# A two-layer hybrid encoder: interleaved softmax factors, tables and fetches moved, pools reordered

## The chip, the cores and the metric

The kernel runs on one NeuronCore of a Trainium2 chip. The metric is the device time of one execution in microseconds (us). Before the change it is 2843.03 us, the median of three runs (2841.9 to 2843.21).

## The reference

Input and output are 2048 × 1024 in float32. Two layers run one after the other, each with a residual. Cut to what matters:

```python
h = rms_norm(x, norm_g); proj = h @ w_in
# layer 0: two attentions over chunks of 64, 8 heads of 64 each
#   A: own chunk + 2 before, rope, a learned sink per head in the softmax
#   B: own chunk + 8 before, a relative-position bias added to the scores
x = x + concat([ya * silu(gate_a), yb * silu(gate_b)]) @ w_out
# layer 1: differential attention, 8 heads, keys up to the query's chunk
a = softmax(q1 @ k1.T * scale) - lam * softmax(q2 @ k2.T * scale)
o = rms_norm(a @ v, subln_g) * (1 - lambda_init)
x = x + (o * silu(gate)) @ w_out
```

## The kernel before, in words

Tokens are worked on in 16 tiles of 128, four of which make a block of 512. Matrix products of float32 quality are made from float32r halves: every operand is split into a high and a low part, and `mm3` (L209 to L217) issues three matmuls, high × high (L214), high × low (L215), low × high (L216). The low part of a weight is a subtraction on GpSimd (POOL, L310); for the first weights of layer 0, half of these subtractions run on VectorE (DVE).

`_project` computes a layer's q, k and v (layer 0: gates too) for two blocks at a time. `hidden` (L315) norms and transposes a block; layer 1 keeps one block in the pool `ev` and one in `hv`. `tables` (L264) loads cos and sin and calls `rope_tables` (L176), eleven DVE instructions (L185 to L193) that fold the gains into them. In layer 1 it is called at the start of the projection. Results go to scratch tensors in DRAM (q, k: L394, L395; v: L483), and the attention loads them again.

`_mix0` runs layer 0's attentions. `scores_a` (A) computes scores, sets masks by memsets (L632 to L634), takes the negated row maximum (L635) and its minimum with the sink (L636), then the exponential on ScalarE (ACT, L640), and adds the sink's term to the row sum (L643). `scores_b` (B) does the same with L716 to L724. The probabilities are transposed on TensorE (PE; L674, L739) into PSUM banks that `split_pt` (L591 on ACT, L592 on DVE) empties into halves, ahead of the products with v (L681, L683, L743, L744). `join` (L595) and `finish` (L602) merge heads and multiply by the gates (L605); `split_y` (L611, L612) splits the result. Some gates of layer 0 are computed in between, by `late_gate` (L775), whose tiles sg and gt share two buffers, tag `xr`, with the residual tiles of `out_tile` (L489). `out_tile` computes an output tile of 128 × 512 and adds the residual on DVE (L504).

`_mix1` runs layer 1's attention. `scores` (L892) works on key chunks of 512 and for both halves of the difference: L913 and L914 (PE), maximum (L917, DVE), exponential (L920, ACT). A row's chunks get factors e (L928) against their common maximum; e is multiplied by the chunk sums la (L929) and summed (L930). GpSimd scales and combines the probabilities (L936, L945, L946), with a part on DVE (L943). `values` (L949) transposes (L959), evacuates (L962 on ACT, L964 on DVE) and multiplies by v (L966). `gate` (L975) norms and gates the result. For the middle blocks o goes to DRAM, and `fetch` (L1016) loads it again (tile coy, L1020) and splits it at once (`split`, L1010: L1012 on ACT, L1013 on POOL). Output tiles: `out_begin` (L1075) loads the residual xr, `out_step` multiplies, `out_end` adds (L1088) and writes (L1089). The four-buffer tag `ot` holds gate outputs, o, coy and xr. `projected_last` does the last block's output, four tiles at a time, k by k.

Each engine runs its instructions in order, and so does SyncE (SP), which issues nearly all DMAs. The order is set when the kernel is built: generators (`pace`, `weave`) emit the heads, the products with v and the side work in turn; a list scheduler with its own timing model then places every instruction on its engine by readiness, and `issue_after` keeps an instruction behind a given one. Tiles come from pools; a tag's number of buffers decides how many lie side by side, and a pool that is opened later lies over one that was closed earlier, in the order of opening: in layer 1's attention `ot`, then `sm`, then `ld` (the q tiles, L888 and L889, and gate weights, L1059).

Of the kernel before, what the change touches and what calls it, by code (L numbers as in the profile page):

```python
# [85 lines left out]
class Trunk:  # L86
# [137 lines left out]
    def _project(self, es, layer):  # L224
# [39 lines left out]
        def tables():  # L264
            if layer == 0:
                self.parameters(xp.tile([P, D], F32, tag="xt", name=n + "tmp"))
            self.cos = xp.tile([P, S // P, 32], F32, tag="xt", name=n + "cos")
            self.sin = xp.tile([P, S // P, 32], F32, tag="xt", name=n + "sin")
# [3 lines left out]
            tabs["q"] = self.rope_tables(tb, self.gain[gq], 0.125, n + "tq")  # L272
            tabs["k"] = self.rope_tables(tb, self.gain[gk], 1.0, n + "tk")
# [145 lines left out]
        for half in range(2):  # L419
# [13 lines left out]
            for gi, (kind, c0, width, o) in enumerate(groups):  # L433
                w = ready or weights(c0, width)
# [54 lines left out]
    def out_tile(self, y, w, j, t, c, xin, xout, sb, pmm, n, tag, xtag="xr", xbufs=None, order=range(KT), after=None):  # L489

        nc = self.nc
        tok, cs = slice(t * P, (t + 1) * P), slice(c * 512, (c + 1) * 512)
        xr = sb.tile([P, 512], F32, tag=xtag, name=n + "xr", bufs=xbufs)
        nc.sync.dma_start(xr, xin[tok, cs])
        ps = pmm.tile([P, 512], F32, tag=tag, name=n + "om")
        for i, k in enumerate(order):
            self.mm3(
                ps, y[k][0][:, j * P:(j + 1) * P], y[k][1][:, j * P:(j + 1) * P],
                w[0][k][c], w[1][k][c], i == 0, i == KT - 1, self.anchor,
            )  # L500
            if after:
                after(i)
            yield 1
        nc.vector.tensor_tensor(xr, ps, xr, ALU.add)  # L504
        nc.sync.dma_start(xout[tok, cs], xr)
        yield 1
# [16 lines left out]
    def _mix0(self, es):  # L523
# [71 lines left out]
        def join(yt, O, e):  # L595
            hi = slice(e * HD, (e + 1) * HD)
            lo = slice((1 - e) * HD, (2 - e) * HD)
            tmp = sb.tile([P, BLK], F32, tag="low", name=n + "low")
            nc.scalar.activation(tmp[hi, :], O[lo, :], AF.Copy)
            nc.vector.tensor_tensor(yt[hi, :], O[hi, :], tmp[hi, :], ALU.add)  # L600
# [14 lines left out]
        def scores_a(h, b, res):  # L615
# [7 lines left out]
            for z in range(2):  # L623
# [12 lines left out]
                nc.vector.tensor_scalar(nm[:, zs], nm[:, zs], self.nsink[:, h:h + 1], None, ALU.min)  # L636
# [117 lines left out]
        def projected(b):  # L754
# [11 lines left out]
            for j, c in units:  # L766
                while next_load(c):
                    pass
                pm, tag = (pO, "O") if b == 0 and j % 2 else (pmm, "om")
                after = follow if b and (j, c) == units[-1] else None  # L770
                yield from self.out_tile(
                    split[b], w, j, b * NTB + j, c, a["x"], self.x1, yp, pm, n, tag, xbufs=2, order=ended, after=after
                )

        def late_gate(b, c, wg, h, r0):  # L775
# [7 lines left out]
            sg = yp.tile([P, BLK], F32, tag="xr", name=n + "sg", bufs=2)  # L783
# [73 lines left out]
    def _mix1(self, es):  # L857
        nc, tc, a, s = self.nc, self.tc, self.a, self.s1
        n = "c"
        pool = lambda nm, bufs, **kw: es.enter_context(tc.tile_pool(name=n + nm, bufs=bufs, **kw))  # L860
        ot = pool("ot", 4)
        sm = pool("sm", 8)
        ld = pool("ld", 2)
        yp = pool("y", 2 * KT)
        vp = pool("v", 4)
        pp = pool("pp", 20)
# [25 lines left out]
        def scores(h, b, q, K, res, then):  # L892
# [4 lines left out]
            for j in range(NTB):  # L897
# [5 lines left out]
                nm, la, e = small("nm", 8), small("la", 8), small("e", 8)  # L903
                nm, la, e = (x.rearrange("p (m z) -> p m z", m=2) for x in (nm, la, e))
                l, rl = small("l", 2), small("rl", 2)
                rows = []
                for m in range(2):
                    chunks = []
                    for z, (c, ce) in enumerate(cuts):
# [10 lines left out]
                        nc.scalar.activation(chunks[z][:, :wd], ps, AF.Exp, bias=nm[:, m, z:z + 1], accum_out=acc)  # L920
# [3 lines left out]
                if nb > 1:  # L924
# [4 lines left out]
                    nc.vector.tensor_tensor(pe, e[:, :, :nb], la[:, :, :nb], ALU.mult)  # L929
# [85 lines left out]

        def fetch(h, b):  # L1016
# [58 lines left out]
        def out_begin(b, j, c):  # L1075
# [3 lines left out]
            pl, tag = (pG, "G") if b < NB - 1 else (pS, "S")  # L1079
# [11 lines left out]
        def projected(b):  # L1091
# [3 lines left out]
            for i, c in enumerate(halves):  # L1095
                for j in range(NTB):
                    xr, ps, to = out_begin(b, j, c)
                    for k in range(KT):
                        out_step(b, j, k, ps, w)
                        if j == NTB - 1 and i == 0:  # L1100
                            load_w(halves[1], k, w[k])
                        elif j == NTB - 1:
                            fetch(k, b + 1)
# [4 lines left out]
        def projected_last():  # L1108
# [15 lines left out]
            for c, w in ((1, w[0]), (0, pairs)):  # L1124
                tiles = [out_begin(b, j, c) for j in range(NTB)]
                for k in range(KT):
                    while (k, b) not in ended:
                        yield 0
                    for j in range(NTB):
                        out_step(b, j, k, tiles[j][1], w)  # L1130
                    yield 1
                for t in tiles:
                    out_end(*t)
# [45 lines left out]
        def side():  # L1179
            yield from gates()  # L1180
            for b in range(NB):
                for h in range(8):
                    while (h, b) not in ended and b < NB - 1:
                        yield 0
                    fetch(h, b)
# [50 lines left out]
```

## Time and profile before

| | |
|---|---|
| median of three runs | 2843.03 us |
| the profiled execution | 2843.39 us |
| its span (first to last instruction) | 2841.6 us |
| TensorE busy | 2707.3 us, 95% |
| VectorE, GpSimd, ScalarE busy | 65%, 56%, 54% |
| mean granted TensorE clock | 0.987 |
| instructions | 43911 |
| moved by DMA | 521.68 MB, mean 184 GB/s |

The profile is one execution. "Busy" counts the time an engine spends in instructions; a stall of one engine is put down to the instruction whose end released it. A matmul that is waited for may run on a clock that the throttle has lowered, which the column of the granted clock shows (1.00 is full speed). In rows of the kind `2.56 POOL L612 ... x2` the first number is a length in us, the line is that of the kernel before, and the tile names are the program's. The stages of the span, by the lines that run in them: layer 0's projection to about 600 us, its attention and output to 1160, layer 1's projection to 1776, layer 1's attention and output to the end.

### The profile page before, as it was taken

To read this page: it belongs to the slowest core of one execution; us is meant where nothing else is said; L and a number is where in the kernel's file an instruction comes from. 1 tells how busy PE (TensorE), PEld (TensorE's weight loads), DVE (VectorE), ACT (ScalarE), POOL (GpSimd) and SP (SyncE) were. 2 spreads that over 40 slices of the span, in tenths; PEclk is the share of its full clock that TensorE was granted. 3 is DMA by queue.
4 is the path that set the end of the run, shared out by engine and by line. 5 is a ranking of instruction groups with operands and counts; after the bars stand their busy time and mean duration, and the time that the engine had idled before them with its cause. 6 is when DMAs were issued, how large, how long until landed. Compare 5 with 4: busy or idle time off the path is not lost.

```text
span 2841.6 us, 43911 instructions
## 1 busy us (share of the span) xinstructions
PE 2707.3 (95%) x13384; PEld 2171.4 (76%) x13384; DVE 1844.8 (65%) x4643; ACT 1543.8 (54%) x4015; POOL 1596.6 (56%) x1740
## 2 busy tenths in 40 slices
PE   7999999999899999899999999899999999999998
PEld 5888888887788888777788888777676777676766
DVE  7752285347788886498808870468787777666651
ACT  4443543367766666243334331468787676666751
POOL 3541252234545454267745560468888887888871
PEclk9999999999999999999999999999999999999999
DMA  5674343738887765476885443887868676464542
GB/s 161 228 233 149 108 140 120 220 117 232 218 197 186 190 181 150 155 271 198 254 255 189 141 126 108 251 251 212 248 187 232 180 212 207 120 191 131 176 137 81
DMA packets 356092, 521.68 MB, mean 184 GB/s; under 512 B 44816, under 2 KB 139792, under 8 KB 355856
## 3 DMA queue, kind: packets, MB, share of 16 engines
q1 hardware_dynamic: 355856, 518.87, 61.6%
q8 instruction: 107, 1.75, 0.3%
q14 instruction: 129, 1.06, 0.1%
HBM read 361.70 MB, written 157.02 MB: 183 GB/s over the span
## 4 chain that ended last, share of the span: by engine, by line
PE 73%; DVE 9%; DMA 9%; ACT 4%; issue 2%; POOL 2%; SPq 1%; DVEq 0%; ACTq 0%; POOLq 0%
PE cO L966 7%; PE p1mm L214 5%; PE p1mm L216 5%; PE p1mm L215 5%; PE cS L913 4%; PE cS L914 4%; PE ctr L959 3%; PE p0mm L214 3%; PE p0mm L216 3%; PE p0mm L215 3%; PE com L214 2%; PE com L215 2%; PE com L216 2%; PE mom L214 2%; PE cG L214 2%
## 5 line engine op out<-in xcount | busy, mean ns | idle before, releaser
L920 ACT ACTIVATE cP<-cS,cnm 128x512 f32<-128x512 f32 (+3 forms) x640 | 397.3, 628 | 181.6 <-DVE cnm L917 142.9
L917 DVE TENSOR_REDUCE cnm<-cS 128x1 f32<-128x512 f32 (+3 forms) x640 | 371.7, 601 | 80.0 <-PE cS L914 74.1
L936 POOL TENSOR_SCALAR cP<-cP,crl,ce 128x512 f32<-128x512 f32 (+3 forms) x288 | 220.0, 778 | 164.2 <-DVE crl L931 84.7
L215 PE MATMUL p1mm<-p1wL,p1hH 128*128 128x512 f32 x768 | 302.3, 394 | 0.4 <-POOL p1wL L310 0.4
L214 PE MATMUL p1mm<-p1wH,p1hH 128*128 128x512 f32 x768 | 301.1, 393 | 0.8 <-ACT p1wH L308 0.8
L216 PE MATMUL p1mm<-p1wH,p1hL 128*128 128x512 f32 x768 | 301.8, 393 | 0.0
L310 POOL TENSOR_TENSOR p0wL<-p0ws,p0wH 128x512 fp32r<-128x512 f32 (+1 forms) x124 | 149.4, 1237 | 266.8 <-ACT p0wH L308 257.8
L966 PE MATMUL cO<-cpt,cv 128*128 128x512 f32 (+3 forms) x640 | 287.7, 537 | 4.2 <-DVE cpt L964 3.6
L946 POOL TENSOR_TENSOR cP<-cP,cP 128x512 f32<-128x512 f32 (+3 forms) x256 | 285.5, 1140 | 1.4
L913 PE MATMUL cS<-ck,cqd 128*128 128x512 f32 (+3 forms) x640 | 261.2, 413 | 12.4 <-ACT cP L920 7.1
L214 PE MATMUL p0mm<-p0wH,p0hH 128*128 128x512 f32 (+1 forms) x640 | 239.9, 377 | 5.2 <-ACT p0vt L472 3.5
L310 POOL TENSOR_TENSOR p1wL<-p1ws,p1wH 128x512 fp32r<-128x512 f32 x128 | 169.2, 1342 | 133.6 <-ACT p1wH L308 126.4
L216 PE MATMUL p0mm<-p0wH,p0hL 128*128 128x512 f32 (+1 forms) x640 | 239.6, 375 | 1.8 <-DVE p0hL L336 1.8
L215 PE MATMUL p0mm<-p0wL,p0hH 128*128 128x512 f32 (+1 forms) x640 | 239.2, 374 | 0.0
L914 PE MATMUL cS<-ck,cql 128*128 128x512 f32 (+3 forms) x640 | 231.4, 367 | 4.4 <-DMA cql<-qL 4.4
L959 PEld LDWEIGHTS ctr<-ident,cP 128*128 128x128 f32 x1088 | 136.8, 141 | 109.7 <-issue 60.8
L945 POOL TENSOR_SCALAR cP<-cP,crl,ce 128x512 f32<-128x512 f32 (+3 forms) x230 | 180.0, 795 | 0.0
L959 PE MATMUL ctr<-ident,cP 128*128 128x128 f32 x1088 | 172.9, 274 | 0.8 <-ACT cpt L962 0.3
L214 PEld LDWEIGHTS p1mm<-p1wH,p1hH 128*128 128x128 f32 x768 | 144.7, 188 | 29.8 <-ACT p1wH L308 1.0
L215 PEld LDWEIGHTS p1mm<-p1wL,p1hH 128*128 128x128 f32 x768 | 144.7, 188 | 29.5 <-POOL p1wL L310 0.8
L216 PEld LDWEIGHTS p1mm<-p1wH,p1hL 128*128 128x128 f32 x768 | 144.7, 188 | 28.8
L913 PEld LDWEIGHTS cS<-ck,cqd 128*128 128x128 f32 x640 | 121.9, 191 | 44.6 <-ACT cP L920 19.9
(306 smaller groups left out, 7271.1 us busy)
## 6 DMA issues: line engine op xcount, KB each, us to landing
p1ws<-in_od_w_in_dram SPq DMA_DIRECT2D x56, 512.0 KB, 4.4
p0ws<-in_ev_w_in_dram SPq DMA_DIRECT2D x48, 512.0 KB, 4.4
ck<-kH SPq DMA_DIRECT2D x144, 128.0 KB, 3.3
ck<-kL SPq DMA_DIRECT2D x144, 128.0 KB, 3.5
cv<-v SPq DMA_DIRECT2D x72, 256.0 KB, 4.5
cqd<-qH SPq DMA_DIRECT2D x128, 128.0 KB, 4.6
cql<-qL SPq DMA_DIRECT2D x128, 128.0 KB, 4.6
cwH<-wgH SPq DMA_DIRECT2D x64, 256.0 KB, 4.6
```

What stands on the lines that cost most here:

```text
L214: mm(ps, aH, bH, start=first, stop=False)
L215: mm(ps, aH, bL, start=False, stop=False)
L216: mm(ps, aL, bH, start=False, stop=last)
L310: low.tensor_tensor(l[:, :width], ws[:, k, :width], f32(h[:, :width]), ALU.subtract)
L913: mm(ps, qd[:, m, js], kt[:, :wd], start=True, stop=False)
L914: self.anchor = mm(ps, ql[:, m, js], kt[:, :wd], start=False, stop=True).ins
L917: nc.vector.tensor_reduce(nm[:, m, z:z + 1], ps, AX.X, ALU.max, negate=True)
L920: nc.scalar.activation(chunks[z][:, :wd], ps, AF.Exp, bias=nm[:, m, z:z + 1], accum_out=acc)
L936: nc.gpsimd.tensor_scalar(p1, p1, rl[:, 0:1], e1, ALU.mult, ALU.mult)
L946: nc.gpsimd.tensor_tensor(p1, p1, p2, ALU.add)
L959: nc.tensor.transpose(tp[:, (j - j0) * P:(j - j0 + 1) * P], us[j][kt // 4][:, kk:kk + P], self.ident)
L966: mm(O[:, j0 * P:], v, T[:, :wd], start=(kt == 0), stop=(kt == nkt - 1), skip_group_check=True)
```

## The change

1. cos and sin lie in tag `xn` of pool `sb` (five buffers), no longer in the x tiles' tag `xt`. In layer 1 the table instructions are held behind the last residual add of layer 0.
2. The first weight group of layer 1 also has half its low parts subtracted on DVE.
3. L636 becomes two instructions of one column each. In layer 0, half of the output tiles of the last block take their residual tile from pool `yt`; sg has a buffer of its own, and `low` has one buffer, not two.
4. In layer 1's attention the pools open in the order `ld`, `sm`, `ot`, and `pp` (probabilities) has 19 buffers, not 20.
5. e and la lie in turn in one tile `el` of 16 columns, and the product is a reduction by multiplication over neighbours, so that it has one operand.
6. A fetched o lies in its own tag `oy` of two buffers; its split comes one fetch later and is held behind the latest exponential.
7. `projected_last` does seven of eight k of the four tiles of c = 1, seven of a tile of c = 0 "ahead", then the eighth k of both; the other three tiles follow one after another.
8. The side work waits for a head's end only where o went through DRAM.

```diff
+            self.cos = sb.tile([P, S // P, 32], F32, tag="xn", name=n + "cos", bufs=5)
...
+            with self.tc.issue_after(self.added) if layer else nullcontext():
+                tabs["q"] = self.rope_tables(tb, self.gain[gq], 0.125, n + "tq")
...
-                w = ready or weights(c0, width)
+                w = ready or weights(c0, width, first=half == gi == 0)
...
-        nc.vector.tensor_tensor(xr, ps, xr, ALU.add)
+        self.added = nc.vector.tensor_tensor(xr, ps, xr, ALU.add).ins
...
-                nc.vector.tensor_scalar(nm[:, zs], nm[:, zs], self.nsink[:, h:h + 1], None, ALU.min)
+                for j in (2 * z, 2 * z + 1):
+                    nc.vector.tensor_scalar(nm[:, j:j + 1], nm[:, j:j + 1], self.nsink[:, h:h + 1], None, ALU.min)
...
-            sg = yp.tile([P, BLK], F32, tag="xr", name=n + "sg", bufs=2)
+            sg = sb.tile([P, BLK], F32, tag="sg", name=n + "sg", bufs=1)
...
+        ld = pool("ld", 2)
+        sm = pool("sm", 8)
         ot = pool("ot", 4)
-        sm = pool("sm", 8)
-        ld = pool("ld", 2)
...
-        pp = pool("pp", 20)
+        pp = pool("pp", 19)
...
+                el = small("el", 16).rearrange("p (m z i) -> p m z i", m=2, i=2)
+                e, la = el[:, :, :, 0], el[:, :, :, 1]
...
-                    nc.vector.tensor_tensor(pe, e[:, :, :nb], la[:, :, :nb], ALU.mult)
+                    nc.vector.tensor_reduce(pe, el[:, :, :nb, :], AX.X, ALU.mult)
...
-                o = ot.tile([P, BLK], F32, tag="ot", name=n + "oy")
+                o = ot.tile([P, BLK], F32, tag="oy", name=n + "oy", bufs=2)
                 nc.sync.dma_start(o, s["o"][h * P:(h + 1) * P, b * BLK:(b + 1) * BLK])
-                split(h, b, o)
+                fetched.append((h, b, o))
+
+        def split_fetched(left):
+            if len(fetched) > left:
+                with tc.issue_after(self.exp):
+                    split(*fetched.pop(0))
...
+            first = [out_begin(b, j, 1) for j in range(NTB)]
+            for k in range(KT - 1):
+                yield from step(range(NTB), first, w[0], k)
+            ahead = [out_begin(b, 0, 0, pG, "G")]
+            for k in range(KT - 1):
+                yield from step((0,), ahead, pairs, k)
+            yield from step(range(NTB), first, w[0], KT - 1)
```

How this moves instructions is shown at three places; line numbers after the change are the same or higher, by up to 35. First, DVE in layer 0's attention A, where manm is the negated maximum, mSA the scores, mal the row sums and mptL a low half of transposed probabilities. Before:

```order
L634 MEMSET mSA 64x2x64
L635 TENSOR_REDUCE manm<-mSA 128x2
L633 MEMSET mSA 64x2x64
L636 TENSOR_SCALAR manm<-manm,nsink 128x2
L643 TENSOR_TENSOR mal<-mal,maes 128x4
L634 MEMSET mSA 64x2x64
L644 RECIPROCAL mar<-mal 128x4
L635 TENSOR_REDUCE manm<-mSA 128x2
L592 TENSOR_TENSOR mptL<-mtrA,mptH 128x384
```

After the change, at the corresponding place:

```order
L636 TENSOR_REDUCE manm<-mSA 128x2
L593 TENSOR_TENSOR mptL<-mtrA,mptH 128x128
L638 TENSOR_SCALAR manm<-manm,nsink 128x1 x2
L634 MEMSET mSA 64x2x64
L645 TENSOR_TENSOR mal<-mal,maes 128x4
L635 MEMSET mSA 64x2x64
L646 RECIPROCAL mar<-mal 128x4
L636 TENSOR_REDUCE manm<-mSA 128x2
L593 TENSOR_TENSOR mptL<-mtrA,mptH 128x384
```

The minimum is two one-column instructions; the sum mal, of two operands, still follows close behind.

Second, DVE at the change of layers: mxr is the residual added to an output tile of layer 0, p1tqC to p1tkS are layer 1's tables. Before:

```order
L592 TENSOR_TENSOR mptL<-mtrB,mptH 128x128
L600 TENSOR_TENSOR myt<-mOB,mlow 64x512
L185 TENSOR_TENSOR p1tqC<-p1cos,od_q_norm 128x16x32
L186 TENSOR_TENSOR p1tqC<-p1cos,od_q_norm 128x16x32
L185 TENSOR_TENSOR p1tkC<-p1cos,od_k_norm 128x16x32
L186 TENSOR_TENSOR p1tkC<-p1cos,od_k_norm 128x16x32
L190 TENSOR_SCALAR p1tqC<-p1tqC 128x1024
L187 TENSOR_TENSOR p1tqS<-p1sin,od_q_norm 128x16x32
L188 TENSOR_TENSOR p1tqS<-p1sin,od_q_norm 128x16x32
L187 TENSOR_TENSOR p1tkS<-p1sin,od_k_norm 128x16x32
L188 TENSOR_TENSOR p1tkS<-p1sin,od_k_norm 128x16x32
L504 TENSOR_TENSOR mxr<-mom,mxr 128x512 x2
```

After the change:

```order
L505 TENSOR_TENSOR mxr<-mom,mxr 128x512
L327 SCALAR_TENSOR_TENSOR p1xt<-p1xt,p1xr,p1g_in 128x1024
L505 TENSOR_TENSOR mxr<-mom,mxr 128x512 x5
L185 TENSOR_TENSOR p1tqC<-p1cos,od_q_norm 128x16x32
L186 TENSOR_TENSOR p1tqC<-p1cos,od_q_norm 128x16x32
L187 TENSOR_TENSOR p1tqS<-p1sin,od_q_norm 128x16x32
L188 TENSOR_TENSOR p1tqS<-p1sin,od_q_norm 128x16x32
L185 TENSOR_TENSOR p1tkC<-p1cos,od_k_norm 128x16x32
L186 TENSOR_TENSOR p1tkC<-p1cos,od_k_norm 128x16x32
L187 TENSOR_TENSOR p1tkS<-p1sin,od_k_norm 128x16x32
L188 TENSOR_TENSOR p1tkS<-p1sin,od_k_norm 128x16x32
L337 TENSOR_TENSOR p1hL<-p1trh,p1hH 128x4x128 x2
```

The tables now come behind all adds of layer 0 and ahead of low halves p1hL of hidden tiles that layer 1's projection multiplies first.

Third, SP at the end of layer 1's projection, where p1v is a finished tile of v and cqd, cql the first q tiles of the attention. Before:

```order
L483 DMA v<-p1v 128x512 x9
L888 DMA cqd<-qH 64x512
L889 DMA cqd<-qH 64x512
L483 DMA v<-p1v 128x512
L888 DMA cql<-qL 64x512
L889 DMA cql<-qL 64x512
```

After the change:

```order
L484 DMA v<-p1v 128x512 x5
L891 DMA cqd<-qH 64x512
L892 DMA cqd<-qH 64x512
L484 DMA v<-p1v 128x512
L891 DMA cql<-qL 64x512
L892 DMA cql<-qL 64x512
```

The q loads stand in the queue four v writes earlier; further down in it, the first gate weights (cwH, cwL) stand ahead of the last v writes too.

More of the change, by code (lines that the diff above doesn't have):

```diff
@@ L769, in projected @@
                 pm, tag = (pO, "O") if b == 0 and j % 2 else (pmm, "om")
+                xp, xt, xb = (yp, "xr", 2) if b or j % 2 else (self.yt, "yt", None)
                 after = follow if b and (j, c) == units[-1] else None
                 yield from self.out_tile(
[L772 removed]
+                    split[b], w, j, b * NTB + j, c, a["x"], self.x1, xp, pm, n, tag, xtag=xt, xbufs=xb, order=ended, after=after
                 )
@@ L1182, in side @@
                 for h in range(8):
-                    while (h, b) not in ended and b < NB - 1:
+                    while (h, b) not in ended and (h, b) not in place:
                         yield 0
-                    fetch(h, b)
+                    if all(f[:2] != (h, b) for f in fetched):
+                        fetch(h, b)
+                if b == NB - 1:
+                    while fetched:
+                        split_fetched(0)
                 yield from projected(b) if b < NB - 1 else projected_last()
```

48 lines of the change are left out of this document (29 added, 19 removed).

## The prediction

> **What bounds the kernel now.** I read the page first, then the busy time of the engines by stage, then what TensorE waited for, and last the lines and moments behind the largest waits. The page gives each engine's busy time and share:
>
> ```profile
> PE 2707.3 (95%) x13384; PEld 2171.4 (76%) x13384; DVE 1844.8 (65%) x4643; ACT 1543.8 (54%) x4015; POOL 1596.6 (56%) x1740
> ```
>
> TensorE is the bound. The diff leaves all but a handful of its instructions as they are, so the change can win only from 2841.6 − 2707.3 = 134.3 us of idle and from stretches at a lowered clock. The busy time by stretch (window, its length, PE, weight loads, DVE, ACT, POOL, granted clock, DMA share, GB/s) shows where that lies:
>
> ```profile
> 600.00:1100.00 500.00, 463.43 (x2887) 406.70 (x2886) 399.15 (x1410) 354.72 (x949) 243.85 (x370) 0.98 0.77 196
> 1100.00:1250.00 150.00, 136.33 (x674) 112.77 (x672) 91.57 (x201) 62.47 (x149) 58.11 (x49) 0.98 0.53 181
> 1250.00:1400.00 150.00, 140.94 (x651) 113.69 (x650) 136.19 (x213) 56.52 (x133) 110.25 (x87) 0.99 0.68 219
> 1750.00:1800.00 50.00, 40.65 (x176) 33.40 (x175) 8.30 (x31) 10.53 (x30) 7.50 (x12) 0.90 0.47 131
> 1800.00:2800.00 1000.00, 972.42 (x4419) 712.42 (x4418) 694.62 (x1736) 674.91 (x1895) 783.67 (x883) 0.99 0.66 191
> ```
>
> Idle: 36.6 us in layer 0's attention (600 to 1100), 13.7 at the change of layers, 9.1 in the next stretch, where DVE is busy 136 of 150 us, 9.4 where layer 1's attention starts, 27.6 in its 1000 us. TensorE's waits (what waited, for whom: us in total, times, longest):
>
> ```profile
> PE mtrB L739 <- DVE mptL L592: 15.6, 17, 3.8
> PE mom L214 <- DVE mxr L504: 8.1, 4, 6.0
> PE cS L914 <- DMA cql<-qL: 4.4, 1, 4.4
> PE com L214 <- ACT cyk L1012: 3.7, 1, 3.7
> PE com L214 <- DVE cxr L1088: 3.6, 2, 2.5
> PE cO L966 <- DVE cpt L964: 3.6, 4, 2.1
> PE com L214 <- ACT cy L1012: 3.1, 2, 2.7
> ```
>
> No single cause holds the time; it is a dozen stalls of 2 to 6 us, and most edits of the diff touch one of them.
>
> A stall costs more than its length. In this stretch two stalls of over 3 us lie (both below), and the granted clock is 0.90:
>
> ```profile
> 700.00:750.00 50.00, 40.12 (x225) 34.53 (x224) 34.43 (x107) 35.70 (x88) 31.07 (x43) 0.90 0.70 168
> ```
>
> A tenth of 50 us at the full clock is 5 us for the two. I count 2 us for each stall of 3 us or more that goes.
>
> **The change part by part.** *The sink's minimum and the row factors (L636, L929).* Totals of the lines (us, then mean ns), and the spread of single instructions (ns: shortest/median/longest):
>
> ```profile
> L929 DVE TENSOR_TENSOR cpe<-ce,cla 128x4 f32<-128x4 f32 (+2 forms) x96 | 54.5, 567 | 48.4 <-ACT ce L928 47.8
> L636 DVE TENSOR_SCALAR manm<-manm,nsink 128x2 f32<-128x2 f32 x64 | 25.3, 398 | 0.3
> L718 DVE TENSOR_SCALAR mbnm<-mbm 128x1 f32<-128x1 f32 x112 | 23.0, 205 | 0.2
> L930 DVE TENSOR_REDUCE cl<-cpe 128x2 f32<-128x4 f32 (+2 forms) x96 | 15.0, 156 | 2.5
> ```
> ```profile
> L636 DVE TENSOR_SCALAR manm<-manm,nsink x64: 149/221/4312, 607.3 to 1096.4; 128x2 f32<-128x2 f32 x64
> L929 DVE TENSOR_TENSOR cpe<-ce,cla x96: 142/168/4146, 1801.3 to 2759.5; 128x4 f32<-128x4 f32 x32, 128x6 f32<-128x6 f32 x32, 128x8 f32<-128x8 f32 x32
> L643 DVE TENSOR_TENSOR mal<-mal,maes x32: 141/158/1298, 610.8 to 1099.1; 128x4 f32<-128x4 f32 x32
> ```
>
> Tiny instructions take up to 4.3 us. At one of them the timeline (start, length) has POOL at work, and TensorE standing:
>
> ```profile
> 734.75 2.56 POOL L612 TENSOR_TENSOR myL<-myt,myH 128x512 fp32r<-128x512 f32 x2
> 735.48 4.31 DVE L636 TENSOR_SCALAR manm<-manm,nsink 128x2 f32<-128x2 f32 x1
> 737.23 1.31 POOL L605 TENSOR_TENSOR myt<-myt,mgt 128x512 f32<-128x512 f32 x1
> 741.45 0.63 PE L739 MATMUL mtrB<-ident,mPB 128*128 128x128 f32 x4 [3.75 <-DVE mptL L592]
> 1043.54 1.34 DVE L636 TENSOR_SCALAR manm<-manm,nsink 128x2 f32<-128x2 f32 x1
> 1044.80 1.30 DVE L643 TENSOR_TENSOR mal<-mal,maes 128x4 f32<-128x4 f32 x1
> 1046.62 0.69 PE L739 MATMUL mtrB<-ident,mPB 128*128 128x128 f32 x2 [2.56 <-DVE mptL L592]
> ```
>
> One-column tensor_scalars (L718) and reductions (L930) show no such waits, and these are the forms that the change uses. So 128 one-column operations take 128 × 0.205 = 26.2 us, as much as the 25.3 now, and what goes is the long waits. They hold 54.5 − 15.0 = 39.5 us on DVE in layer 1 and 25.3 − 64 × 0.221 = 11.2 in layer 0. TensorE lost 3.75 + 2.56 us beside the two shown, with 2 for the clock 8.3. But L643, behind L636 on DVE, takes two operands and waited 1.30 us itself: where POOL is still at work it may inherit the wait. I take −4, bounds −9 (both stalls and a smaller one) and +2 (inherited, with the extra instructions ahead of mptL). In layer 1, DVE is busy 69% and TensorE idle only 27.6 us in 1000, so most of the 39.5 us is hidden by scores computed ahead; −3, bounds 0 and −8.
>
> The Trainium skill ("SBUF — State Buffer", Who interferes with whom) says that DVE's second port pair is shared with GpSimd, that a DVE instruction with two SBUF inputs or in a two-port mode is fully blocked while the other holds it for the whole instruction, and that a reduction never contends on trn2. The medians and longest times above agree with who is blocked. They differ on how long: one instruction of POOL is 1.3 us here, and L636 waited through at least three in a row. If a wait ended with one instruction, the term would be 1.3 rather than 4 us.
>
> *The gate's buffer (L786).* The chain of waits at 700:
>
> ```profile
> 698.67 1.26 POOL mgt L789
> 699.95 2.54 DMA g<-mgt
> 702.57 0.63 ACT msg L786
> ```
> ```profile
> 704.47 0.44 PE L739 MATMUL mtrB<-ident,mPB 128*128 128x128 f32 x2 [3.50 <-DVE mptL L592]
> ```
>
> sg waits for the xr buffer that an earlier gate's write still reads; ACT stands in order behind it. With a buffer of its own it doesn't: −3.5 − 1 (half of the clock's share, since smaller waits follow at once) = −4.5, bounds −6 and 0.
>
> *The change of layers (L264, L504).* The chain of waits there:
>
> ```profile
> 1148.59 0.69 DVE p1tqC L185
> 1154.13 0.70 DVE mxr L504
> ```
>
> Nine table instructions (0.6 us each) stand ahead of the add that frees a PSUM bank; TensorE waits 6.0 us for it (the mxr row). The new order puts all tables behind the last add: −6 − 2 = −8. They don't vanish: 11 × 0.6 = 6.6 us, with four of L310's subtractions moved from POOL to DVE, land where DVE is the busiest.
>
> ```profile
> L310 DVE TENSOR_TENSOR p0wL<-p0ws,p0wH 128x512 fp32r<-128x512 f32 x4 | 3.9, 986 | 6.9 <-ACT p0wH L308 6.9
> ```
>
> That is 6.6 + 3.9 = 10.5 us into a DVE with 14 us free in 150. Some of it fits into its idle before 1200; I give back 3, bounds 0 and 10.5.
>
> *The start of layer 1's attention (pools, L888 to L889).* SyncE issues the first q loads so late because their tiles lie over weights of the projection; TensorE stands twice, 4.1 us for cqd's load and then the 4.4 for cql of the list above:
>
> ```profile
> 1738.90 32.96 SPq L483 DMA_DIRECT2D v<-p1v  x7
> 1776.33 0.45 SPq L888 DMA_DIRECT2D cqd<-qH  x1
> ```
> ```profile
> 1780.36 0.45 PE L913 MATMUL cS<-ck,cqd 128*128 128x128 f32 x1 [4.10 <-DMA v<-p1v]
> ```
>
> With ld first, the tiles lie over the hidden blocks that are last read four token tiles before the end. A v write comes every 33/6 = 5.5 us, so the loads go out some 22 us earlier and have landed by the time the matmuls want them. −4.1 − 4.4 − 2 = −10.5; I take −10 for what is next late (the v loads), bounds −13 and −4.
>
> *The fetch of y (L1012, L1020, L1088).* In layer 1 the chain has waits of TensorE behind loads:
>
> ```profile
> 2457.66 4.75 DMA coy<-o
> ```
> ```profile
> 2712.66 5.13 DMA cxr<-x
> ```
>
> coy and xr take turns in four ot buffers, and the split (ACT, POOL) stands in their queues from the moment of the load. The new tag and the deferred split remove ACT's waits for the load; behind them were cpt's 2.1, cy's 2.7 and cxr's 2.5 us. Two of three gone with a little of the clock: −6, bounds −10 and +3 (the last when a split comes so late that the output's first products wait for it, one cy wait more).
>
> *Start and tail.* In the first 100 us DVE's tables, fed by a load issued earlier, only trade places with other DVE work: 0, bounds ±3. At the tail TensorE waits 3.7 us for cyk; behind it now 87 instead of 108 products are left, but the 21 that were taken ahead stand before the last values, where TensorE has no idle. So they shift the wait and don't fill it: 0, bounds −4 (they do fill it) and +2. pp at 19 instead of 20 buffers: 0, hidden by scores that run ahead; up to +3 if not.
>
> **Sum.** −4 − 3 − 4.5 − 8 + 3 − 10 − 6 = −32.5. The whole order is planned anew, and the 134 us hold some 100 us of small waits that are dealt afresh; where one input comes sooner another is next late. I hold back 7.5 us, about a quarter: −25. The profiled execution took 2843.39 us, 1.8 more than its span and 0.4 over the median of 2843.03, so either gives 2818.
>
> **The rivals.** *Only the loads' stalls go (2828):* the blocked time of DVE is hidden or inherited by the next instruction with two operands, and the splits gain nothing: −10 − 8 + 3 = −15. For it: L643's row; L929's 39.5 us against little idle. Against: 15.6 us behind mptL.
>
> *All stalls go (2798):* 3.75 + 2.56 + 3.5 + 6.0 + 8.5 + 7.3 = 31.6, the five of 3 us or more with 2 us of clock each, and the 3 of L929: −45. Against: L643 stands ready to inherit one, and 10.5 us come upon DVE.
>
> *Slower (2854):* SyncE's queue is in order. The new order puts q and gate loads ahead of the last four v writes. If their tiles come free only with the end of the projection, they hold these writes back, v has three buffers, and TensorE stops for up to 4 × 5.5 = 22 us with 4 for the clock, and the gain of 10 is lost: −25 + 10 + 26 = +11. It decides when the tiles are free later than about 22 us before the projection's end. Against: the last reader of the hidden block is the fourth tile from the end.
>
> *No change (2843 ± 5.7):* waits go and as many new ones come, DVE's added 10.5 us above all.
>
> **How the numbers follow.** Forecast 0.60, loads only 0.18, all 0.08, slower 0.08, no change 0.06. The forecast's own range is 2803 to 2831: below, the sum without what I held back and with both of L636's stalls gone and more of the clock (−40); above, with L636, L929 and the fetch at nothing (−25 + 4 + 3 + 6 = −12). The range takes in "loads only" with the whole 10.5 us given back in DVE's stretch (2828 + 7.5, and 2 for pp), and leaves out most of the last three cases: 2802 to 2838. A measurement of this kernel tells 0.2%, 5.7 us. Faster: 0.60 and 0.18 nearly whole, with 0.08: 0.84. Same: 0.06 and 0.02 of their edges: 0.08. Slower: 0.08.
>
> **What would show it.** Right: no DVE instruction of L636's or L929's successors over 0.5 us; tables behind the last add and no 6 us wait of mom; no 4 us waits at the first cS and a clock near 1.00 there; no ACT wait for coy. Wrong: DVE near 50 of 50 us after 1190 with new TensorE waits for p1eL or p1xms of over 5 us; L643 at 4 us; v writes late by more than 6 us; new waits for P0's or y's buffers in layer 1.

## The result, and the profile after

The changed kernel takes 2855.58 us (median of 7 runs, 2851.85 to 2862.74). The runs of before beside it have a median of 2840.51 us (2827.63 to 2843.21). The ratio is 1.0059, with a 95% interval of 1.0045 to 1.0073: about 17 us slower. The forecast was 2818 us, 25 us faster. The profiled execution of the changed kernel has a span of 2851.4 us.

TensorE's work is the same; the page says so (busy time and share of each engine):

```profile
PE 2707.5 (95%) x13384; PEld 2174.8 (76%) x13384; DVE 1815.8 (64%) x4711; ACT 1544.3 (54%) x4015; POOL 1581.3 (55%) x1736
```

Its idle time has moved. The same stretches of the changed kernel as in the prediction (window, length, PE, weight loads, DVE, ACT, POOL, granted clock, DMA share, GB/s):

```profile
600.00:1100.00 500.00, 468.63 (x2948) 413.87 (x2948) 402.08 (x1508) 355.80 (x963) 244.97 (x377) 0.99 0.78 198
1100.00:1250.00 150.00, 135.68 (x645) 111.93 (x644) 94.84 (x190) 61.57 (x140) 59.67 (x43) 0.97 0.59 196
1250.00:1400.00 150.00, 142.34 (x655) 115.45 (x654) 133.21 (x208) 56.01 (x130) 111.86 (x88) 0.99 0.69 223
1750.00:1800.00 50.00, 49.34 (x235) 40.23 (x234) 21.99 (x82) 22.99 (x73) 19.05 (x28) 1.00 0.77 221
1800.00:2800.00 1000.00, 946.92 (x4251) 693.24 (x4250) 662.06 (x1682) 659.54 (x1846) 761.53 (x867) 0.98 0.63 184
```

Layer 0's attention has 5 us less idle time, and the start of layer 1's attention almost none, at the full clock. But in the 1000 us of that attention TensorE stands for 53.1 us, where it stood for 27.6. So the loss is in the last row alone.

Two waits of before that the prediction left out (what waited, for whom: us in total, times, longest):

```profile
PE cS L913 <- ACT cP L920: 7.1, 11, 1.3
...
PE cG L214 <- DMA cwH<-wgH: 4.2, 3, 1.8
```

And TensorE's waits in the changed kernel:

```profile
PE cS L917 <- ACT cP L924: 18.9, 23, 3.5
...
PE cG L214 <- DMA cwH<-wgH: 13.4, 4, 6.6
...
PE ctr L965 <- DVE cP L949: 6.6, 1, 6.6
PE com L214 <- DVE cxr L1103: 6.3, 3, 3.6
...
PE p1trh L332 <- DVE p1xms L205: 4.9, 1, 4.9
...
PE com L214 <- ACT cyk L1018: 3.7, 1, 3.7
...
PE mom L214 <- DVE mxr L505: 2.7, 2, 2.0
```

The score's wait for an exponential (a PSUM bank that ACT has not emptied) has become the longest list entry, and a wait for gate weights the third. The 6.0 us wait at the change of layers is down to 2.0. The wait of 6.6 us for L949, which is L943 before the change, is new. Its instruction and its neighbours in the changed kernel (ns: shortest/median/longest):

```profile
L638 DVE TENSOR_SCALAR manm<-manm,nsink x128: 141/198/215, 600.7 to 1080.1; 128x1 f32<-128x1 f32 x128
L645 DVE TENSOR_TENSOR mal<-mal,maes x32: 135/162/1577, 603.8 to 1082.9; 128x4 f32<-128x4 f32 x32
L935 DVE TENSOR_REDUCE cpe<-cel x96: 133/161/171, 1776.7 to 2770.1; 128x4 f32<-128x8 f32 x32, 128x6 f32<-128x12 f32 x32, 128x8 f32<-128x16 f32 x32
L949 DVE SCALAR_TENSOR_TENSOR cP<-cP,cc,cP x58: 518/986/8674, 1779.4 to 2773.9; 128x512 f32<-128x512 f32 x43, 128x384 f32<-128x384 f32 x6, 128x256 f32<-128x256 f32 x5, 128x128 f32<-128x128 f32 x4
```

and before:

```profile
L943 DVE SCALAR_TENSOR_TENSOR cP<-cP,cc,cP x58: 350/884/1594, 1802.8 to 2763.3; 128x512 f32<-128x512 f32 x43, 128x384 f32<-128x384 f32 x6, 128x256 f32<-128x256 f32 x5, 128x128 f32<-128x128 f32 x4
```

The new forms of L636 (now L638) and L929 (now L935) never wait: 215 and 171 ns at most. The longest L943, an instruction of two large operands, went from 1.6 to 8.7 us. The timeline of the changed kernel there:

```profile
2399.68 3.02 POOL L942 TENSOR_SCALAR cP<-cP,crl,cel 128x512 f32<-128x512 f32 x4
2400.49 8.67 DVE L949 SCALAR_TENSOR_TENSOR cP<-cP,cc,cP 128x512 f32<-128x512 f32 x1 [1.75 <-POOL cP L942]
2402.69 2.26 POOL L951 TENSOR_SCALAR cP<-cP,crl,cel 128x512 f32<-128x512 f32 x3
2404.91 3.70 POOL L952 TENSOR_TENSOR cP<-cP,cP 128x512 f32<-128x512 f32 x3
2409.22 0.69 PE L965 MATMUL ctr<-ident,cP 128*128 128x128 f32 x2 [6.64 <-DVE cP L949]
2409.86 0.69 ACT L924 ACTIVATE cP<-cS,cnm 128x512 f32<-128x512 f32 x1 [10.74 <-DVE cnm L921]
```

GpSimd runs these ten instructions without a gap, nine of them within L949's 8.67 us. VectorE is held, the maxima behind it come late, ACT idles 10.7 us for them, and TensorE 6.6.

The time can be split by milestones. Layer 1's first score starts at 1780.4 us before and at 1760.6 after. From there to the end of the span are 1061.2 and 1090.8 us. So in these two executions the change wins 19.8 us ahead of layer 1's attention and loses 29.6 in it. That is 9.8 us net, where the timed runs say 17, and the 19.8 is more than usual: among the profiles of all kernels in the table below, the six with the old code up to that point have the first score at 1770.1 to 1780.4 us (median 1775.8), the twelve with the new code at 1759.8 to 1770.0 (median 1764.3). The usual win is about 11.5 us. The experiments split the loss.

### The profile page after: what moved, and what is told of

It reads as the page before. It is cut to its first block, busy times and chain, and to the rows that moved or that the text cites. A ratio compares the mean times of both kernels' runs of the same rounds, so it can differ in the third digit from the quotient of the medians.

```text
span 2851.4 us, 43980 instructions
## 1 busy us (share of the span) xinstructions
PE 2707.5 (95%) x13384; PEld 2174.8 (76%) x13384; DVE 1815.8 (64%) x4711; ACT 1544.3 (54%) x4015; POOL 1581.3 (55%) x1736
## 4 chain that ended last, share of the span: by engine, by line
PE 72%; DVE 10%; DMA 8%; ACT 4%; issue 3%; POOL 2%; SPq 1%; DVEq 0%; ACTq 0%; POOLq 0%
PE cO L972 7%; PE p1mm L215 5%; PE p1mm L214 4%; PE p1mm L216 4%; PE cS L917 4%; PE cS L918 3%; PE ctr L965 3%; PE p0mm L214 3%; PE p0mm L216 3%; PE p0mm L215 3%; PE com L214 2%; PE com L215 2%; PE com L216 2%; PE mom L214 2%; PE mom L216 2%
## 5 line engine op out<-in xcount | busy, mean ns | idle before, releaser
L942 POOL TENSOR_SCALAR cP<-cP,crl,cel 128x512 f32<-128x512 f32 (+3 forms) x288 | 218.4, 772 | 197.9 <-DVE crl L937 73.9
L917 PE MATMUL cS<-ck,cqd 128*128 128x512 f32 (+3 forms) x640 | 262.8, 415 | 19.0 <-ACT cP L924 18.9
L951 POOL TENSOR_SCALAR cP<-cP,crl,cel 128x512 f32<-128x512 f32 (+3 forms) x230 | 173.2, 763 | 0.0
```

Source lines behind the costliest of these rows:

```text
L917: mm(ps, qd[:, m, js], kt[:, :wd], start=True, stop=False)
L942: nc.gpsimd.tensor_scalar(p1, p1, rl[:, 0:1], e1, ALU.mult, ALU.mult)
```

## The experiments

Each kernel is compared with the kernel before on the same chip. "Attention" is the time from layer 1's first score to the end of the span, and "exp waits" the total of the wait of cS for cP, both from the profiled execution; the ratio is that of the timed runs.

| run | buffers | ratio (95%) | first score, us | attention, us | exp waits, us |
|---|---|---|---|---|---|
| before | 20 | 1 | 1780.4 | 1061 | 7.1 |
| changed kernel | 19 | 1.0059 (1.0045 to 1.0073) | 1760.6 | 1091 | 18.9 |
| e1 factors only | 20 | 1.0012 (0.9995 to 1.0030) | 1780.0 | 1064 | 6.6 |
| e2 changed, no factors | 19 | 1.0040 (1.0024 to 1.0056) | 1770.0 | 1087 | 22.6 |
| e3 changed, no fetch | 19 | 1.0064 (1.0045 to 1.0084) | 1759.8 | 1086 | 17.3 |
| e4 front and pools | 19 | 1.0025 (1.0009 to 1.0040) | 1766.8 | 1079 | 23.2 |
| e5 front only | 20 | 0.9984 (0.9968 to 1.0000) | 1769.7 | 1064 | 6.7 |
| e6 front and order | 20 | 0.9948 (0.9931 to 0.9966) | 1763.3 | 1058 | 7.6 |
| e7 before, 19 buffers | 19 | 1.0079 (1.0053 to 1.0105) | 1775.3 | 1079 | 19.4 |
| e8 order of pools only | 20 | 1.0000 (0.9984 to 1.0017) | 1766.9 | 1058 | 9.2 |
| e9 changed, 20 buffers | 20 | 0.9998 (0.9982 to 1.0013) | 1767.2 | 1073 | 9.8 |
| e10 front, order, factors | 20 | 0.9980 (0.9965 to 0.9995) | 1762.9 | 1062 | 7.2 |
| e11 front, order | 21 | 0.9956 (0.9943 to 0.9969) | 1768.0 | 1064 | 16.4 |
| e12 before, 18 buffers | 18 | 1.0094 (1.0070 to 1.0118) | 1770.1 | 1091 | 25.0 |
| e13 before, lead 32 | 19 | 1.0056 (1.0035 to 1.0077) | 1776.3 | 1072 | 17.1 |
| e14 before, lead 32 | 20 | 1.0007 (0.9989 to 1.0024) | 1774.8 | 1060 | 10.2 |
| e15 changed, lead 32 | 19 | 0.9990 (0.9975 to 1.0004) | 1766.3 | 1068 | 11.8 |
| e16 front, order, fetch | 20 | 0.9989 (0.9977 to 1.0002) | 1764.7 | 1067 | 10.7 |
| e17 front, order, small tiles 5 | 20 | 0.9950 (0.9932 to 0.9967) | 1760.8 | 1061 | 7.2 |
| e18 front, order, new tail | 20 | 0.9968 (0.9951 to 0.9985) | 1763.8 | 1064 | 8.7 |

"Buffers" are those of the pool `pp`. The profiled execution is one sample, and a kernel's runs spread by up to 0.7%, so small differences are read from the ratios only.

**First: the factors, the fetch, and layer 1's pools.** The theories were that the wait for GpSimd moves from L929 to L943 and costs more there (1), that the fetch costs (2), or that any change re-deals the order (3).

e1 has part 5 of the change alone, e2 all but it:

```diff
-                    nc.vector.tensor_tensor(pe, e[:, :, :nb], la[:, :, :nb], ALU.mult)
+                    nc.vector.tensor_reduce(pe, el[:, :, :nb, :], AX.X, ALU.mult)
```

> The kernel before, with only the interleaved factors and the product by a reduction (L929). Theory 1 (the wait for GpSimd moves from L929's tiny product to the next two-operand instructions of VectorE, L943, L993 and L995, which then stop the scores): slower than before by 4 to 15 us, and L943's longest instruction rises from 1.6 us to over 4. Theory 2 (the new fetch and its late split cost the time in layer 1): within 4 us of before. Theory 3 (any change in layer 1 re-deals its small waits): anywhere within 10 us, without a longer L943.

> The changed kernel with the factors as before (two tiles, a product of two operands), all else changed. Theory 1: faster than the changed kernel by 8 to 20 us, to about 2835 to 2847, L943's successor back at 1.6 us at most and L929 again up to 4 us. Theory 2: within 4 us of the changed kernel, 2851 to 2859. Theory 3: within 10 us of it, either way.

e3 takes back the deferred fetch and the new waits of the side work (parts 6 and 8); e4 is the kernel before with parts 1 to 4.

```diff
-                fetched.append((h, b, o))
+                split(h, b, o)
```

> The changed kernel with the fetch and its split as before (shared buffers, split at once, the old waits of the side work), all else changed. Theory 1: within 5 us of the changed kernel, and the two-operand instructions still up to 8 us long. Theory 2: faster by 10 to 25 us, to 2831 to 2846. Theory 3: within 10 us of it, either way.

> The kernel before with the changes of layer 0, of the change of layers and of layer 1's pools only; layer 1's attention code is as before. In the changed kernel's trace layer 1's attention starts 20 us sooner. Theories 1 and 2: that gain is kept to the end, 2818 to 2826. Theory 3 or a cost of the pools (19 buffers, order of the pools): layer 1's attention loses part of it again, 2828 to 2845.

e1: the longest L943 is 8.7 us, as theory 1 has it, but the ratio's interval holds no change. e2: the changed kernel without the factors is 0.2% faster than with them (the intervals overlap), less than theory 1 wanted, and L943 still takes up to 6.0 us. So the wait can move, and it is not the main loss. e3 gives nothing back: theory 2 fails as the main cause. e4 has none of the new attention code, yet its attention is 17 us longer than before. The loss is in the pools or in how the order is planned anew.

**Second: which part of the pools.** Part 4 is the order of the pools and one buffer fewer.

```diff
-        pp = pool("pp", 20)
+        pp = pool("pp", 19)
```

> The kernel before with the changes of layer 0 and of the change of layers only; layer 1's pools and attention as before. Its first score of layer 1 should come about 8 to 12 us sooner than before. Theory P (the pools of layer 1, order or number, lengthen its attention by 15 to 25 us): attention as long as before, 1058 to 1066 us from the first score to the end, total 2826 to 2834 on the scale of the profiled 2843. Theory R (whatever moves the times ahead of layer 1 re-deals the order in it): attention longer by 8 or more, total 2838 to 2846.

> As the run with front and pools, but 20 probability buffers, not 19; the pools still in the new order. Theory P with the number of buffers as the cause: attention 1060 to 1066 us, the score's waits for an exponential back from 22 us to about 7, total 2822 to 2830. Theory P with the order of pools as the cause, or theory R: as that run, attention 1074 to 1083 us.

> The kernel before with 19 probability buffers, not 20, and nothing else. If the number of buffers is the cause: attention 8 to 15 us longer, the score's waits for an exponential at 15 us or more. If not: within 4 us of before.

> The kernel before with layer 1's pools in the new order (20 buffers) and nothing else. The two 4 us waits of the first scores should be gone: attention starts 8 to 10 us sooner in terms of its end. If the order of pools costs the loads of gate weights their place: those waits rise from 4 to 11 us or more, total within 4 us of before. If only other changes re-deal the order: 8 to 12 us faster than before.

e7 is before with this one line changed, and it is 0.79% slower, 22 us. e6 is e4 with this one line taken back, and it is 0.77% faster than e4. The number of buffers is the cause of the loss; that any change ahead of layer 1 re-deals its order (e5) is refuted, its attention is 1064 us. e6, 0.52% faster than before, beats both kernels. e8's ratio is 1, though its profiled execution is shorter (it is the fastest of its ten runs); its 14 us head start on the profile of before is not confirmed by the timed runs.

How such a loss looks: the chain of waits of e7 (start, length, what),

```profile
2566.62 5.78 DVE cP L943
2572.40 0.61 DVE cnm L917
...
2573.04 0.78 ACT cP L920 x2
```

and TensorE's timeline at its end:

```profile
2573.87 0.33 PE L913 MATMUL cS<-ck,cqd 128*128 128x128 f32 x1 [3.97 <-ACT cP L920]
```

It is a wait of L943 for GpSimd, as in the changed kernel, but in a kernel that has the old factors. The wait alone is not the loss. e8, with the old factors and 20 buffers, has one as long, and TensorE's longest wait for an exponential is 1.4 us (first the spread of L943 in ns, then TensorE's wait):

```profile
L943 DVE SCALAR_TENSOR_TENSOR cP<-cP,cc,cP x58: 465/990/6061, 1785.7 to 2746.5; 128x512 f32<-128x512 f32 x43, 128x384 f32<-128x384 f32 x6, 128x256 f32<-128x256 f32 x5, 128x128 f32<-128x128 f32 x4
```
```profile
PE cS L913 <- ACT cP L920: 9.2, 16, 1.4
```

The same holds for the other kernels with the old factors and a long L943 (5.7 to 6.2 us). In the 10 us after its start TensorE waits for exponentials 1.1 to 1.4 us with 20 or 21 buffers (e5, e8, e11) and 2.7 to 4.5 us with 19 (e2, e4, e7). Nor is it the only way to lose the time: in e12 below, with 18 buffers, the longest L943 is 1.7 us, and the exp waits are 25.0.

**Third: the changed kernel with the buffer back, and more or fewer.** e9 takes the memory from the small tiles; e10 to e12 follow from e6 and before.

```diff
-        sm = pool("sm", 8)
+        sm = pool("sm", 5)
...
-        pp = pool("pp", 19)
+        pp = pool("pp", 20)
```

> The changed kernel with 20 probability buffers again (the memory is taken from the small per-row tiles, 5 buffers each, not 8). If the one buffer is the cause: about 22 us faster than the changed kernel, ratio to before 0.996 to 1.001, and layer 1's attention, from the first score to the end, at 1060 to 1070 us, not 1091. If the factors, the fetch and the tail cost the time: ratio 1.004 or more, attention over 1078 us.

> The kernel with front and order (20 buffers) and the interleaved factors, nothing else. If the wait for GpSimd moves to the next two-operand instruction at a cost: slower than the run without by 4 to 12 us (ratio 0.996 to 0.999 to before), and the longest L943 over 4 us. If it is hidden either way: ratio 0.993 to 0.996, as without.

> Front and order with 21 probability buffers. If each buffer sets how far the scores run ahead: a further 5 to 20 us faster than with 20, ratio 0.988 to 0.993, attention under 1053 us. If 20 suffice and only the nineteenth to twentieth matters: ratio 0.993 to 0.997.

> The kernel before with 18 probability buffers. If each buffer is one chunk of scores of lead: another 12 to 25 us above 19 buffers, ratio 1.012 to 1.017. If 19 was an unlucky number (the buffers' turn no longer in step with the four chunks of a row): no slower than 19, ratio 1.008 or less.

e9 is level with before: the buffer is worth 1.0059 − 0.9998 = 0.61%, 17 us, in the changed kernel; its attention, 1073 us, is 18 us shorter. But e9 is 0.5% behind e6, so other parts cost too. e10 shows one: factors on top of e6 cost 0.32%, 9 us, though the two intervals just touch. The longest L943 without and with the factors:

```profile
L946 DVE SCALAR_TENSOR_TENSOR cP<-cP,cc,cP x58: 465/989/2231, 1782.2 to 2741.5; 128x512 f32<-128x512 f32 x43, 128x384 f32<-128x384 f32 x6, 128x256 f32<-128x256 f32 x5, 128x128 f32<-128x128 f32 x4
```
```profile
L947 DVE SCALAR_TENSOR_TENSOR cP<-cP,cc,cP x58: 467/888/8696, 1782.6 to 2744.8; 128x512 f32<-128x512 f32 x43, 128x384 f32<-128x384 f32 x6, 128x256 f32<-128x256 f32 x5, 128x128 f32<-128x128 f32 x4
```

21 buffers win nothing over 20, and 18 cost little more than 19 (1.0094 lies between e12's two ranges, and its interval reaches into the second, so an unlucky number is not excluded). It is a step between 20 and 19, not a slope. (e11's exp waits, 16.4 us at the ratio of 0.9956, also show that this column alone does not price a kernel.)

**Fourth: how the missing buffer acts, and the fetch.** The generators plan the scores of the last two blocks 36 units ahead of the products with v (`LAG1`). A chunk of 512 keys is two units for each half of the difference, and the pool holds the first halves only, so one buffer is worth four units.

```diff
-    BANKS1, LAG1 = (4, 2, 1, 1), (30, 30, 36, 36)
+    BANKS1, LAG1 = (4, 2, 1, 1), (30, 30, 32, 32)
```

> The kernel before with 19 probability buffers and, for the last two blocks, the scores planned 32 units ahead of the products with v, not 36 (a probability buffer holds a chunk of one half, four units with its partner). If 19 buffers cost because the plan asks for more lead than they hold: most of the loss comes back, ratio 0.998 to 1.004. If the lead itself is what is missing: ratio 1.007 or more, as with 19 and 36.

> The control: 20 buffers, as before, with 32 units of lead. If lead itself is what 19 buffers take away: slower than before by 10 to 25 us, ratio 1.004 to 1.009. If plan and buffers out of step are the cause: ratio 0.997 to 1.003.

> The changed kernel (19 buffers) with 32 units of lead. If plan and buffers out of step are the cause: 10 to 20 us faster than the changed kernel, ratio 0.999 to 1.003. If the lead itself: ratio 1.005 or more.

> Front and order with 20 buffers, and the new fetch with its late split (5 buffers for the small tiles, to make room), no factors and no new tail. If the fetch wins its 6 us as forecast: ratio 0.991 to 0.994. If it wins nothing: 0.994 to 0.997, as without. If it costs: 0.997 or more.

e14: four units less of lead with 20 buffers cost nothing, so the planned lead itself is not what is missing. e15: with the lead that fits 19 buffers, the changed kernel gains 0.7%, 20 us, and loses all of its deficit. Both fit a plan and buffers out of step. e13 does not bear this out: 1.0056 in place of 1.0079, between its two ranges, with intervals that overlap. So the missing buffer is shown as the cause of 17 to 22 us. That plan and buffers were out of step is the likely way, but it is not shown, since the kernel before recovers little with the shorter lead. A rival that no run tests is the turn of the buffers: by the kernel's text, the 16 tiles of a head of the last block and the four of the next head's first row make just 20.

e16 has the fetch with its late split and the new waits of the side work (parts 6 and 8), and is 0.41% behind e6, so they seemed to cost 12 us. It had cut the small tiles as well; e17 makes that cut alone. e18 does the tail alone.

> Front and order with 20 probability buffers and 5 buffers for the small per-row tiles, not 8, nothing else: it parts the fetch from the room made for it. If the small tiles cost the time of the run with the fetch: ratio 0.998 to 1.001. If the fetch did: 0.993 to 0.997, as front and order alone.

> Front and order with 20 buffers and the new order of the last block's output tiles (seven eighths, then a tile ahead), nothing else. As forecast, the tile ahead stands where TensorE has no idle: ratio 0.993 to 0.997, as without, and the wait for cyk at the tail still 3.7 us. If it fills the wait: 4 us faster, 0.992 to 0.994, the wait under 1 us.

The small tiles cost nothing, hence the fetch did: e16 is 0.39% behind e17, and the intervals are apart. The late split hardly shortens ACT's wait for the load, from 14.9 us in e17 to 13.4 in e16:

```profile
ACT cy L1015 <- DMA coy<-o: 14.9, 7, 4.5
```
```profile
ACT cy L1017 <- DMA coy<-o: 13.4, 5, 5.7
```

SyncE's rows of e16 show why. The first two fetched tiles are loaded 530 us or more ahead and hold both buffers of `oy` until their split at 2441.6 us; the third load goes out only behind it:

```profile
1877.15 0.32 SPq L1027 DMA_DIRECT2D coy<-o  x1
1909.18 0.32 SPq L1027 DMA_DIRECT2D coy<-o  x1
2449.11 1.56 SPq L1027 DMA_DIRECT2D coy<-o  x2
```

TensorE's wait for cy is gone, 1.8 us in e17. But its waits for gate weights (cwL) rose from 1.3 to 3.9 us, for exponentials from 7.2 to 10.7 and for cxr from 2.7 to 4.3. What makes these later is not shown. e18 is at 0.9968; its interval overlaps e6's, and the wait at the tail is still there:

```profile
PE com L214 <- ACT cyk L1015: 3.7, 1, 3.7
```

## Why the prediction was wrong, point by point

The stages are compared here in two ways: between the two profiled executions, and between all of this case's profiles, seven with the old code ahead of layer 1 (before, e1, e7, e8, e12 to e14) and thirteen with the new. The second comparison shows which differences repeat.

**Start, 0.** Layer 0's first scores start at 598.3 us, and at 604.9 before: −6.6 us, more than the bound of 3. It repeats: 603.5 to 605.9 us in the seven, 596.3 to 601.6 in the thirteen. The term was put at nothing, and no run shows which part of the change wins it.

**L636 and the gate's buffer, −4 and −4.5.** From those scores to the last product with v (mOB), 535.8 us before and 526.2 after: −9.6 against −8.5. This agreement is luck. The seven took 526.3 to 535.8 us (median 529.5), the thirteen 525.0 to 532.7 (median 527.5): about −2. The long L636 that the prediction priced, 4.31 us, has its like only in e1 (3.9); in the other five with the old code the longest is 1.3 to 1.4. And the rival that L643 inherits the wait came true in four of the thirteen, though not in the changed kernel's own profile (1.6 us at most). In e2, e4, e5 and e11 its successor L645 takes up to 3.6 to 4.5 us, and TensorE's longest wait for mptL is 3.6 to 4.5 us, against 0.9 to 2.1 in the other nine. In e4:

```profile
L645 DVE TENSOR_TENSOR mal<-mal,maes x32: 134/162/4226, 603.0 to 1086.4; 128x4 f32<-128x4 f32 x32
```
```profile
PE mtrB L741 <- DVE mptL L593: 10.1, 14, 4.1
```

**The change of layers, −8 and +3 back.** From there to the first transposes of layer 1's projection it took 48.5 us before and 42.7 after: −5.8 (medians 48.9 and 44.4). The projection itself took 586.6 us before and 593.1 after: +6.5 (medians 586.6 and 593.6), within the bound of 10.5. What was moved was paid for in full, where a net −5 was forecast: TensorE's longest wait for p1xms rose to 4.9 us.

**The start of layer 1's attention, −10.** To the end of the first head (the first L995), −9.7. It repeats: 66.4 to 68.7 us in the seven profiles with the old order of pools, 56.0 to 58.9 in the thirteen with the new. SyncE's rows show it: the first q load goes out 21 us ahead of the projection's last matmul (1760.3 us), where it came 0.4 behind it before, and the last v write is not late.

```profile
1738.98 0.45 SPq L891 DMA_DIRECT2D cqd<-qH  x1
...
1755.98 0.32 SPq L484 DMA_DIRECT2D v<-p1v  x1
```

Together these are −25.3 us at the end of layer 1's first head (1843.9 and 1818.6); the prediction's terms for them sum to −23.5. This half was right in direction, not in size. The six profiles with all of the old code up to there have a median of 1838.5, the twelve with all of the new 1821.8: −16.7, and of that some 6 us are the start, which was put at nothing. The timed runs of e6, which has just these parts, say −0.52%, 15 us. Part of the start's gain may be handed on behind it: TensorE's waits for gate weights (cwH and cwL) are 7.7 to 13.5 us in the profiles with the new order of pools, 1.4 to 9.6 with the old. The "slower" rival, in which SyncE's queue holds back the v writes, did not occur.

**pp at 19 buffers: "0, hidden by scores that run ahead; up to +3 if not".** This step failed. It measured +17 us in the changed kernel (e9) and +22 on the kernel before (e7). The prediction priced the buffer by TensorE's waits of before, in which the pool does not appear at all. With 20 buffers the scores' waits for exponentials are 7.1 us, and nothing in that trace says that 19 will not do. What could have warned is a count: a head of the last block has 16 such tiles, which come free only as its products with v go on, and a lead of 36 units wants nine more. It does not give the step, though. The sum is 25, and 24 with a lead of 32, yet 21 buffers win nothing over 20. Why the step lies between 19 and 20 stays open.

**L929, −3.** It measured +0.1% (e1) to +0.3% (e10), 3 to 9 us. None of e1, e2 and e10 is clear of the noise alone; all three point the same way. The kind of wait was right, and the prediction named an heir in layer 0 (L643). It did not look for one in layer 1: L943 stands a few instructions behind L929, has two operands of 512 columns, and keeps the maxima behind it waiting. L929's blocked time had let GpSimd get ahead before L943 came; without it VectorE reaches L943 while GpSimd is in the middle of a row. The last sentence is argued from the order of the two, not shown by a run of its own; shown is that the longest L943 is 8.7 us in e1, e3, e9, e10 and the changed kernel, which have the factors, and 1.6 to 6.2 in those without. In those five, TensorE's transposes then wait 4.8 to 6.7 us for it. In total VectorE gains: in the changed kernel L929's successor takes 15.4 us (54.5 before), and the 58 long L943 take 73.2 (54.9 before). So the cost can only lie in where the wait falls. In e15, with the factors and a lead of 32, the longest L943 is 2.6 us, so the handing on depends on the order too.

**The fetch, −6.** It measured +11 to +12 us (e16 against e17 and e6), and nothing in the changed kernel (e3). The step "the new tag and the deferred split remove ACT's waits for the load" failed: they are 16.5 us before, 19.7 in the changed kernel and 13.4 in e16, since two buffers let only two loads go ahead of a split. Of the stalls counted as theirs only cy's went; those for cxr and cpt did not shrink (2.7 to 4.3 and 7.5 to 8.2 us, e17 to e16).

**The tail, 0.** Right as far as the runs tell: the 3.7 us wait is unchanged, and e18's ratio overlaps e6's.

**What was held back, +7.5.** Meant for waits dealt afresh. In layer 1's attention the price was 17 us for the buffer and about 14 for the rest (e9 against e6), where −9 was forecast.

## What to carry to other kernels

A buffer taken from a pool that feeds the bounding engine is a change of its own: hold the planned lead against the number of tiles before pricing it at zero, and try it alone, since a trace in which the buffers suffice shows nothing of it. A blocked instruction that is made unblockable can hand its wait to the next one on that engine that can be blocked; price the heir, above all if it is a large one with the bound's feeders queued behind it. A stall seen once in one profile may be rare: the 4.3 us of L636 have their like in one of six other profiles, so look at several executions before pricing it. Gains at a stage's start stay only if the stage behind isn't lengthened by a companion edit: here some 15 us were won (e6, 0.52% faster than before) and some 30 lost (the changed kernel against e6, 1.1%).

## What the runs showed of the hardware

GpSimd can hold a VectorE instruction over many of its own. The rows above show L949 held from 2400.49 to 2409.16 us while nine GpSimd instructions ran back to back. The Trainium skill ("SBUF — State Buffer", Who interferes with whom) says that the one that issues first holds the shared ports for the whole instruction; here a hold lasted over many instructions, up to 8.7 us. But it is not always so. In the kernel before, L636 went on after 1.34 us, at 1044.88 us, with GpSimd's next instruction right behind:

```profile
1042.35 3.72 POOL L612 TENSOR_TENSOR myL<-myt,myH 128x512 fp32r<-128x512 f32 x3
```
```profile
1043.54 1.34 DVE L636 TENSOR_SCALAR manm<-manm,nsink 128x2 f32<-128x2 f32 x1
```

What decides between the two is not shown. An instruction that reduces over neighbours by multiplication (L935, 96 times) took 133 to 171 ns with GpSimd busy for 762 of 1000 us; the two-operand product took up to 4.1 us before, with GpSimd busy for 784.
